# A gated delta-rule mixer: norm weight moved from the weights to the tokens, decay mask made additive, Silu in pairs, weight subtraction on GpSimd

## The chip, the cores and the metric

The kernel runs on one core of one Trainium2 chip. Its time is device microseconds of one execution of the whole program; the figure compared is the median over the timed executions. The core has TensorE (PE, matrix multiply, with a separate row for its weight loads, PEld), VectorE (DVE), ScalarE (ACT), GpSimd (POOL) and SyncE (SP, which here issues DMAs).

## What is computed

One inference step of a two-layer decoder for 1040 prompt tokens (16 of them learned meta tokens) and 8 single-token samples. Layer A is a gated delta-rule mixer and a convolutional feed-forward, layer B a latent attention and another feed-forward. The change is in the mixer of layer A:

```python
h = rmsnorm(x, a_norm_pre)                      # y * w, w one weight per channel
proj = h @ w_in                                 # q, k, v (each through conv4 and silu), z, a, b
gc = cumsum(g)                                  # per chunk
decay = exp(where(causal, gc[:, None] - gc[None, :], -inf))
strict = where(i > j, (beta k) @ k.T * decay, 0)
u, w = triangular_solve(1 + strict, [beta v, beta k exp(gc)])
attn = (q @ k.T) * decay
# recurrence over chunks: v_new = u - w S;  o = q exp(gc) S + attn v_new;  S = S exp(g_last) + k_tail.T v_new
o = rmsnorm(o, a_out_norm) * silu(z);  out = o @ w_out
```

## The kernel before

All matrix products of activations and weights are done in three passes on split numbers: a high half rounded for TensorE and a low half, the rest. `wprep` (L155) loads a 1024x128 weight tile by DMA into one staging buffer, and `wsplit` (L141) multiplies it by the norm weight on GpSimd where a fold is asked for (L144), rounds it on ScalarE (L151) and subtracts on VectorE (L152) to get the low half. The tokens are normalised by their root mean square without the weight at the start (L215), turned channel-major and split in the same way (L219 to L224); they stay on the chip as xh and xl.

The mixer has 8 heads. For each head there are four weight tiles, k, v, q and z (numbers 1, 2, 0, 3 in the list `tiles`, L161), each projected for three pieces of the tokens of 280, 384 and 384 columns. The order in the list is k, v, q of a head and then z of the head before. `inproj` (L493) projects a tile into one of two PSUM buffers (L93), ScalarE copies it out, and for k, v, q VectorE adds the four taps of the convolution (L546). When the third piece is there, `silu` (L133) is called for that one tile: the scalar engine loads the Silu table (L135), runs it, and loads the table of logarithm and exponential again (L131).

The z tiles of the heads but the last lie in a pool with a single buffer (L383, L507):

```python
zp = es.enter_context(tc.tile_pool(name="gz", bufs=1, reuse_waits="tile"))
...
y = zp.tile([P, T], F32, tag="z", name="z")
```

`chunks` (L560) does what a head needs before the recurrence, in nine chunks of 116 tokens in groups of three. It loads the cumulated decay of all tokens of a chunk on every partition (GC), and makes E, the decay matrix: subtract the own column and take the minimum with zero on VectorE (L581, once per chunk), exponential on ScalarE (L582, once per group), and multiply by the upper triangular mask of ones on GpSimd (L583). Then come the products of keys (L601) and U (L604), whose diagonal blocks go to DRAM and back. The blocks of 32 are inverted by substitution in 31 steps of two small VectorE instructions, a product and a difference (L658, L660), each waiting for the one before; the result goes over DRAM into X, is turned (L668 to L670), and the rest of the head's products follow from L680 on.

`recur` (L734) walks the nine chunks of a head in order. Per group of three it normalises the output and turns it (L770 to L778), multiplies by z (L782), and after the last group it does the 8 samples, which read the first columns of z at L825 ("og8"). That is the last reader of the z buffer. The outputs go to DRAM and are multiplied by the output weights at the end (`tail_a`, `outp`).

The streams are merged by a position number (`merge`, L834): head h's projections stand at h to h+1, its chunks at h+0.65 to h+1.9, its recurrence at h+1.9 to h+2.55, and the instructions are traced in that order. The framework then fixes the order of each engine's instructions when it compiles: earlier traced work first, among what it takes to be ready by its own estimate of times and of free buffers. A buffer is given to a new tile only when the last reader of the old one has been placed, wherever that reader was traced. In the run each engine takes its instructions strictly in that fixed order. `keep_in_program_order` pins an instruction behind the one traced before it on its engine.

Of the kernel before, what the change touches and what calls it, by code (L numbers as in the profile page):

```python
# [20 lines left out]
P = 128  # L21
# [40 lines left out]
def tile_step(ctx: ExitStack, tc: tile.TileContext, I, O, stop=None):  # L62
# [41 lines left out]
    def rsqrt(dst, src, scale, n=P):  # L104
        """dst = (src * scale + EPS)^-0.5"""
        A.activation(dst, src, AF.Ln, bias=epst[:n], scale=scale)
        A.activation(dst, dst, AF.Exp, scale=-0.5)
# [9 lines left out]
    # per-channel vectors as columns  # L117
# [15 lines left out]
    def silu(*ts):  # L133
        for t in ts:
            A.activation(t, t, AF.Silu)  # L135
        act_set()
# [4 lines left out]
    def wsplit(pool, st, kt, m, fold, tag, out=None):  # L141
# [10 lines left out]
        V.tensor_tensor(lo, st, hi, op=ALU.subtract)  # L152
        return hi, lo

    def wprep(pool, src, kt, m, fold=None, tag="w", out=None):  # L155
        st = pool.tile([P, KT * P], F32, tag=tag + "s", name="ws", bufs=1)[:, :kt * m].rearrange("p (k m) -> p k m", k=kt)
        SP.dma_start(st, src)
        return wsplit(pool, st, kt, m, fold, tag, out)
# [3 lines left out]
    for h in range(H):  # L162
        tiles += [(h, 1), (h, 2), (h, 0)] + ([(h - 1, 3)] if h else [])
# [3 lines left out]
    def prep(n):  # L167
        if n < len(tiles) and n not in prepped:
            h, ti = tiles[n]
            col = 1024 * ti + P * h  # L170
            prepped[n] = wprep(wg, I["a_w_in"][0, :, col:col + P].rearrange("(k p) m -> p k m", p=P), KT, P, fold="a_pre")

    A.preload_act_table_set("natural_log_exp_and_others")
    with tc.tile_pool(name="init", bufs=2, reuse_waits="tile") as ip, \
# [4 lines left out]
        def params(spec, conv):  # L179
            r0 = r = 8 if len(vcol) else 0  # L180
# [4 lines left out]
            if conv:  # L185
                A.dma_start(arow, I["a_conv_w"][0].rearrange("j (t p) -> (j t) p", p=P))
            pt = ipp.tile([P, 2, P], F32, name="pt", bufs=1)
            PE.transpose(pt[:, 0, :r], rows[:r, :], ident[:r, :r])
            V.tensor_copy(vec[:, r0:r], pt[:, 0, r0:r])
            if conv:  # L190
                PE.transpose(pt[:, 1, :96], arow, ident[:96, :96])
                V.tensor_copy(acv, pt[:, 1, :96])

        # tokens to channel-major, normalised
        for bi, (t0, n) in enumerate(BLK):
            xt = ip.tile([P, D], F32, name="xt", bufs=4)
            load_tokens(xt, bi)
            if bi == 1:
                params([("a_pre", I["a_norm_pre"][0], 8)], False)
# [3 lines left out]
            elif bi == 8:  # L203
# [6 lines left out]
                ], True)  # L210
# [4 lines left out]
            V.tensor_scalar(xt[:n], xt[:n], ss[:n], None, op0=ALU.mult)  # L215
# [19 lines left out]
    def stat(pp, aps, n, dst, dim):  # L235
        """dst[p, t] = (sum over channels / dim + eps)^-0.5 on every partition."""
# [10 lines left out]
    def boundary(pp, wide, c, wname, split=True, halves=False, store=False):  # L247
        """x <- x + acc * rstd * w for one chunk, kept in acc and, as halves, in xh and xl; the old x is in them or in x_d."""
# [51 lines left out]
    def outp(w, src_d, groups, pool, p0, p1, first=False, skip=0, ob=4):  # L300
        """Shares of an output projection, summed in acc, without the first skip tokens; a group is its heads and where
        their weights go."""
# [45 lines left out]
    # ------------------------------------------------------------------ layer A mixer  # L348
# [1340 lines left out]
```

## Time and profile before

| | us |
|---|---|
| median of 3 runs | 3347.21 |
| lowest and highest | 3346.63, 3354.2 |
| span of the profiled execution, first to last instruction | 3338.6 |
| median less that span | 8.6 |

The runs give no separate time for the profiled execution, so its span stands for it; the 8.6 us are what lies around the instructions. Times in the rows below are microseconds from the start of the span. The mixer runs from 0 to about 850 us, and the feed-forward of layer A follows. TensorE's own busy time is counted from modelled ends of pipelined matmuls. The chain that ended last is given by the page as TensorE 77%, VectorE 14%, DMA 3%, issue 3%, ScalarE 2%, GpSimd 1%.

### The profile page before, as it was taken

How to read it: one execution, taken by the hardware profiler on the slowest of the kernel's cores; microseconds unless marked ns; L12 is line 12 of the kernel's file. 1: busy time of each engine (PE TensorE's matmuls, PEld its weight loads, DVE VectorE, ACT ScalarE, POOL GpSimd, SP SyncE). 2: the span in 40 equal slices, each digit the busy share in tenths (PEclk: the TensorE clock that was granted, in tenths of full speed). 3: DMA queues.
4: the chain of work that ended last, by engine and by line, in shares of the span. 5: the costliest groups of instructions: out<-in, count | busy, mean ns of one | idle time of the engine just before them, and what ended most of it. 6: DMA issues, size and time to landing. Idle time of an engine off the chain costs nothing.

```text
span 3338.6 us, 52527 instructions
## 1 busy us (share of the span) xinstructions
PE 3151.7 (94%) x20846; PEld 2874.7 (86%) x20846; DVE 2031.4 (61%) x4139; ACT 1255.9 (38%) x2541; POOL 860.2 (26%) x1013
## 2 busy tenths in 40 slices
PE   7999999999899999999888999999998999999997
PEld 6888888888699999999877888856677999999996
DVE  4877777766854555555666666544457455655556
ACT  4656555663432222222334444433224322222223
POOL 1432222210442223222431001112104323322322
PEclk9999999999899999999999999999999999999999
DMA  3222222236311111111121000255432111111111
GB/s 109 59 72 71 59 64 69 69 105 184 93 52 39 52 51 45 46 39 55 48 79 39 25 19 27 65 214 195 155 107 77 52 45 45 45 41 56 45 39 65
DMA packets 267649, 235.08 MB, mean 70 GB/s; under 512 B 57918, under 2 KB 246596, under 8 KB 263284
## 3 DMA queue, kind: packets, MB, share of 16 engines
q1 hardware_dynamic: 260224, 189.69, 19.7%
q0 software_dynamic: 6912, 41.95, 3.4%
q8 instruction: 164, 2.69, 0.3%
q14 instruction: 81, 0.66, 0.1%
q10 hardware_dynamic: 268, 0.09, 0.0%
HBM read 198.84 MB, written 33.40 MB: 70 GB/s over the span
## 4 chain that ended last, share of the span: by engine, by line
PE 77%; DVE 14%; DMA 3%; issue 3%; ACT 2%; POOL 1%; SPq 0%; ACTq 0%; DVEq 0%; POOLq 0%
PE fps L228 9%; PE fps L229 9%; PE fps L227 9%; PE fdn L228 5%; PE fdn L227 5%; PE fdn L229 5%; PE psu L227 2%; PE psu L229 2%; PE po L1409 2%; PE psu L228 2%; PE dscr L1494 2%; DVE acc L287 2%; DVE xs L660 1%; DVE tm L658 1%; PE psop L227 1%
## 5 line engine op out<-in xcount | busy, mean ns | idle before, releaser
L144 POOL TENSOR_TENSOR ws<-ws,vec 128x1024 f32<-128x1024 f32 (+1 forms) x127 | 247.6, 1950 | 433.4 <-DMA ws<-in_f_w_up_dram 173.2
L228 PE MATMUL fps<-xfl,wh 128*128 128x384 f32 (+1 forms) x1056 | 343.7, 326 | 8.3 <-POOL xfl L295 8.3
L227 PE MATMUL fps<-xfh,wh 128*128 128x384 f32 (+1 forms) x1056 | 341.7, 324 | 8.0 <-ACT xfh L293 7.0
L228 PE MATMUL fps<-xbl,wh 128*128 128x384 f32 (+1 forms) x1056 | 342.5, 324 | 6.1 <-POOL xbl L295 6.1
L229 PE MATMUL fps<-xfh,wl 128*128 128x384 f32 (+1 forms) x1056 | 342.4, 324 | 0.0
L227 PE MATMUL fps<-xbh,wh 128*128 128x384 f32 (+1 forms) x1056 | 340.6, 323 | 1.1 <-ACT xbh L293 0.5
L229 PE MATMUL fps<-xbh,wl 128*128 128x384 f32 (+1 forms) x1056 | 340.2, 322 | 0.0
L966 DVE TENSOR_TENSOR fu<-fps,RS 128x384 f32<-128x384 f32 x176 | 98.1, 557 | 386.7 <-PE fps L229 386.2
L151 ACT CAST wh<-ws 128x1024 fp32r<-128x1024 f32 (+1 forms) x144 | 148.0, 1028 | 488.1 <-PE fps L228 374.0
L227 PE MATMUL fdn<-gh,dh 128*128 128x384 f32 (+1 forms) x960 | 315.8, 329 | 0.0
L228 PE MATMUL fdn<-gl,dh 128*128 128x384 f32 (+1 forms) x960 | 311.9, 325 | 0.0
L229 PE MATMUL fdn<-gh,dl 128*128 128x384 f32 (+1 forms) x960 | 309.0, 322 | 0.0
L1044 DVE TENSOR_TENSOR acc<-acc,fdn 128x384 f32<-128x384 f32 (+1 forms) x432 | 216.9, 515 | 108.5 <-PE fdn L229 107.7
L227 PE MATMUL psu<-xah,wh 128*128 128x384 f32 (+1 forms) x768 | 261.2, 340 | 11.3 <-ACT u L533 7.0
L228 PE MATMUL psu<-xal,wh 128*128 128x384 f32 (+1 forms) x768 | 259.1, 337 | 0.4 <-DVE xal L223 0.4
L229 PE MATMUL psu<-xah,wl 128*128 128x384 f32 (+1 forms) x768 | 258.7, 337 | 0.7 <-DVE wl L152 0.7
L975 DVE SCALAR_TENSOR_TENSOR fy<-fu,fcv,fy 128x1064 f32<-128x1064 f32 x176 | 238.6, 1358 | 7.5 <-ACT fy L973 7.3
L152 DVE TENSOR_TENSOR wl<-ws,wh 128x1024 fp32r<-128x1024 f32 (+1 forms) x144 | 173.7, 1206 | 70.3 <-ACT wh L151 70.1
L228 PEld LDWEIGHTS fps<-xfl,wh 128*128 128x128 f32 x1056 | 200.8, 190 | 10.7 <-POOL xfl L295 10.5
L227 PEld LDWEIGHTS fps<-xfh,wh 128*128 128x128 f32 x1056 | 200.4, 190 | 9.4 <-ACT xfh L293 7.9
L228 PEld LDWEIGHTS fps<-xbl,wh 128*128 128x128 f32 x1056 | 199.6, 189 | 8.0 <-POOL xbl L295 7.7
L229 PEld LDWEIGHTS fps<-xfh,wl 128*128 128x128 f32 x1056 | 200.8, 190 | 0.4
(963 smaller groups left out, 7857.1 us busy)
## 6 DMA issues: line engine op xcount, KB each, us to landing
ws<-in_f_w_up_dram SPq DMA_DIRECT2D x88, 512.0 KB
ds<-in_f_w_down_dram SPq DMA_DIRECT2D x44, 512.0 KB
ws<-in_a_w_in_dram SPq DMA_DIRECT2D x32, 512.0 KB
xt<-in_x_prompt_dram SPq DMA_DIRECT2D x16, 512.0 KB
of<-og_d SPq DMA_DIRECT2D x32, 192.0 KB
xr<-x_d SPq DMA_DIRECT2D x16, 384.0 KB
GC<-gcd SPq DMA_DIRECT2D x24, 174.0 KB
Ss<-in_state_delta_S_dram SPq DMA_DIRECT2D x8, 512.0 KB
```

What stands on the lines that cost most here:

```text
L144: G.tensor_tensor(st, st, bc(fo, [P, kt, m]), op=ALU.mult)
L151: A.copy(hi, st)
L152: V.tensor_tensor(lo, st, hi, op=ALU.subtract)
L227: PE.matmul(ps, wh, ah, start=start, stop=False)
L228: PE.matmul(ps, wh, al, start=False, stop=False)
L229: PE.matmul(ps, wl, ah, start=False, stop=stop)
L287: V.scalar_tensor_tensor(a_[:, k + j, :], a_[:, k + j, :], vc(wname, k + j), res[j], op0=ALU.mult, op1=ALU.add)
L966: V.tensor_tensor(u[:, 18 + t0:18 + t0 + n], ps[:, :n], RS[:, t0:t0 + n], op=ALU.mult)
L975: V.scalar_tensor_tensor(y, u[:, j:j + LW], fcv[:, l, j, tl:tl + 1], y, op0=ALU.mult, op1=ALU.add)
L1044: V.tensor_tensor(acc[c][:, m, :], acc[c][:, m, :], ps[:, :n], op=ALU.add)
L1409: PE.matmul(po[:, :nq], vt[:kk, kb, P * (h % 2):P * (h % 2) + P], pT[:kk, j, :nq], start=(kb == 0), stop=(kb == i))
L1494: PE.matmul(sc[32 * j:32 * j + 32, :], ql[:, k, b, :], cT[:, j, :], start=(k == 0), stop=False, tile_position=(0, 32 * j))
```

## The change

The norm weight is loaded once on every partition (512 KB) and multiplied into the tokens together with the root mean square. The weight tiles are no longer multiplied, and for the mixer's projections the low half is subtracted on GpSimd. The two calls for parameters become one. The decay mask is added (0 or -1e30) on GpSimd before the exponential, and the own column is subtracted as the bias of the exponential, which is therefore run once per chunk; VectorE has no part in it. The tiles are ordered k, z of the head before, v, q. Silu is called for two tiles at a time, the later tile first, and the second pinned behind the first. The first head's q and the last z are alone. A negated copy of gc is kept in place of gc. Comments were removed as well.

```diff
     def silu(*ts):
-        for t in ts:
-            A.activation(t, t, AF.Silu)
+        for i, t in enumerate(ts):
+            ins = A.activation(t, t, AF.Silu)
+            if i:
+                tc.keep_in_program_order(ins)
         act_set()
...
         A.copy(hi, st)
-        V.tensor_tensor(lo, st, hi, op=ALU.subtract)
+        (sub or V).tensor_tensor(lo, st, hi, op=ALU.subtract)
...
-        tiles += [(h, 1), (h, 2), (h, 0)] + ([(h - 1, 3)] if h else [])
+        tiles += [(h, 1)] + ([(h - 1, 3)] if h else []) + [(h, 2), (h, 0)]
...
-            prepped[n] = wprep(wg, I["a_w_in"][0, :, col:col + P]..., KT, P, fold="a_pre")
+            prepped[n] = wprep(wg, I["a_w_in"][0, :, col:col + P]..., KT, P, sub=G)
...
+        pre = ip.tile([P, D], F32, name="pre", bufs=1)
+        A.dma_start(pre, I["a_norm_pre"][0].partition_broadcast(P))
...
-                params([("a_pre", I["a_norm_pre"][0], 8)], False)
                 prep(0)
...
-            V.tensor_scalar(xt[:n], xt[:n], ss[:n], None, op0=ALU.mult)
+            V.scalar_tensor_tensor(xt[:n], xt[:n], ss[:n], pre[:n], op0=ALU.mult, op1=ALU.mult)
...
-    triu = gp.tile([C, C], F32, name="triu")
-    SP.dma_start(triu, I["c_triu"])
+    umask = gp.tile([C, C], F32, name="umask")
+    SP.dma_start(umask, I["c_umask"])
...
-    gc = gp.tile([C, NCK, H], F32, name="gc")
+    ngc = gp.tile([C, NCK, H], F32, name="ngc")
...
-        wh, wl = wprep(wg, I["a_w_in"][0, :, 4096:4112]..., KT, 16, fold="a_pre",
+        wh, wl = wprep(wg, I["a_w_in"][0, :, 4096:4112]..., KT, 16,
...
+        triu = rp.tile([C, C], F32, tag="tm", name="triu")
+        SP.dma_start(triu, I["c_triu"])
...
+        gc = part(440, C, 72).rearrange("p (a b) -> p a b", b=H)
         V.tensor_copy(gc, ps1[:C])
+        V.tensor_scalar(ngc, ps1[:C], -1.0, None, op0=ALU.mult)
...
+    waiting = []
+
+    def finished(t, alone=False):
+        waiting.insert(0, t)
+        if len(waiting) == 2 or alone:
+            silu(*waiting)
+            waiting.clear()
...
                 if c == 2:
-                    silu(y)
+                    finished(y, h == H - 1)
...
             if c == 2:
-                silu(y[:, :LC])
+                finished(y[:, :LC], h == 0 and ti == 0)
...
+            G.tensor_tensor(E[:, gs, :], GC[:C], umask.unsqueeze(1).to_broadcast([C, 3, C]), op=ALU.add)
             for i in range(3):
                 k = 3 * g + i
-                V.tensor_scalar(E[:, k, :], GC[:C, i, :], gc[:, k, h:h + 1], 0.0, op0=ALU.subtract, op1=ALU.min)
-            A.activation(E[:, gs, :], E[:, gs, :], AF.Exp)
-            G.tensor_tensor(E[:, gs, :], E[:, gs, :], triu.unsqueeze(1).to_broadcast([C, 3, C]), op=ALU.mult)
+                A.activation(E[:, k, :], E[:, k, :], AF.Exp, bias=ngc[:, k, h:h + 1])
             A.activation(GC, GC, AF.Exp)
...
+    c["c_umask"] = np.where(np.triu(np.ones((C, C))) > 0, 0.0, -1e30).astype(f)
```

## Rows read from the trace of the kernel before

**Rows 1.** The page, part 1: busy microseconds of each engine, share of the span, instructions

```profile
PE 3151.7 (94%) x20846; PEld 2874.7 (86%) x20846; DVE 2031.4 (61%) x4139; ACT 1255.9 (38%) x2541; POOL 860.2 (26%) x1013
```

**Rows 2.** Busy time by stretch: one head of the first mixer, after the column line

```profile
core 0: us, PE busy (x) PEld busy (x) DVE busy (x) ACT busy (x) POOL busy (x), PEclk, DMA share, GB/s
439.00:527.00 88.00, 80.11 (x625) 74.03 (x626) 65.57 (x196) 51.19 (x145) 24.62 (x40) 0.96 0.25 67
```

**Rows 3.** Waits of TensorE, 90 to 700 us: total, times, longest

```profile
PE psot L778 <- DVE tm L658: 19.6, 4, 4.9
...
PE psr L680 <- DVE Tt L668: 5.3, 2, 3.0
PE pskt L596 <- DVE Kh L592: 5.0, 5, 2.0
PE pso L823 <- DVE o L820: 3.6, 5, 0.8
PE psot L778 <- DVE on L775: 3.4, 2, 2.3
```

**Rows 4.** Groups by line, 0 to 870 us: xcount, busy us, mean ns, idle before

```profile
L144 POOL TENSOR_TENSOR ws<-ws,vec 128x1024 f32<-128x1024 f32 (+1 forms) x36 | 68.9, 1914 | 185.3 <-DMA ws<-in_a_w_in_dram 87.3 <-DMA og_d<-og 37.1 <-DVE acc L336 36.8
L660 DVE TENSOR_TENSOR xs<-xs,tm 108x84 f32<-108x84 f32 (+23 forms) x248 | 66.8, 269 | 2.8
...
L152 DVE TENSOR_TENSOR wl<-ws,wh 128x1024 fp32r<-128x1024 f32 x38 | 46.3, 1220 | 16.8 <-ACT wh L151 16.7
...
L135 ACT ACT_TABLE_LOAD x32 | 41.1, 1283 | 0.6
...
L581 DVE TENSOR_SCALAR E<-GC,gc 116x116 f32<-116x116 f32 x72 | 32.9, 464 | 0.2 <-DMA GC<-gcd 0.2
...
L583 POOL TENSOR_TENSOR E<-E,triu 116x348 f32<-116x348 f32 x24 | 27.3, 1136 | 12.0 <-ACT E L582 12.0
...
L770 ACT ACTIVATE sqo<-pso 116x128 f32<-116x128 f32 x72 | 19.9, 276 | 31.8 <-PE pso L760 31.2
...
L582 ACT ACTIVATE E<-E 116x348 f32<-116x348 f32 x24 | 11.7, 487 | 18.6 <-DVE E L581 18.6
...
L215 DVE TENSOR_SCALAR xt<-xt,ss 128x1024 f32<-128x1024 f32 (+1 forms) x9 | 6.6, 745 | 5.5 <-ACT ss L107 5.5
```

**Rows 5.** Groups by line, 900 to 1300 us, in the feed-forward

```profile
L975 DVE SCALAR_TENSOR_TENSOR fy<-fu,fcv,fy 128x1064 f32<-128x1064 f32 x48 | 65.3, 1366 | 3.2 <-ACT fy L973 3.1
...
L1007 POOL TENSOR_TENSOR gl<-fy,gh 128x1040 fp32r<-128x1040 f32 x12 | 29.2, 2435 | 3.8 <-ACT gh L1004 3.8
```

**Rows 6.** Timeline of VectorE in that head: start, us, instruction

```profile
453.09 0.19 DVE L658 TENSOR_TENSOR tm<-ins,xs 108x31 f32<-108x31 f32 x1
...
458.18 1.98 DVE L581 TENSOR_SCALAR E<-GC,gc 116x116 f32<-116x116 f32 x1
...
484.73 0.21 DVE L825 SCALAR_TENSOR_TENSOR og<-pso,vec,z 128x8 f32<-128x8 f32 x1
...
490.82 0.16 DVE L660 TENSOR_TENSOR xs<-xs,tm 108x11 f32<-108x11 f32 x1
...
500.54 0.46 DVE L668 STREAM_TRANSPOSE Tt<-X 32x288 f32<-32x288 f32 x1
```

**Rows 7.** Timeline of GpSimd at the same place

```profile
458.14 1.94 POOL L144 TENSOR_TENSOR ws<-ws,vec 128x1024 f32<-128x1024 f32 x1
```

**Rows 8.** Timeline of TensorE there, idle time before in brackets

```profile
467.74 0.81 PE L778 MATMUL psot<-ident,on 116*128 116x116 f32 x3 [4.82 <-DVE tm L658]
...
468.60 0.43 PE L228 MATMUL psu<-xal,wh 128*128 128x280 f32 x1
...
473.52 0.29 PE L229 MATMUL psu<-xah,wl 128*128 128x280 f32 x1
```

**Rows 9.** Timeline of ScalarE there

```profile
455.67 0.37 ACT L533 COPY u<-psu 128x272 f32<-128x272 f32 x1
...
490.31 0.39 ACT L522 COPY z<-psu 128x280 f32<-128x280 f32 x1 [1.13 <-PE psu L229]
```

More of the change, by code (lines that the diff above doesn't have):

```diff
@@ L139, in vc, with wsplit @@
         return vec[:, vcol[nm] + k:vcol[nm] + k + 1]
-    def wsplit(pool, st, kt, m, fold, tag, out=None):
+    def wsplit(pool, st, kt, m, fold, tag, out=None, sub=None):
         if fold is not None:
@@ L151, in wsplit, with wprep @@
         A.copy(hi, st)
-        V.tensor_tensor(lo, st, hi, op=ALU.subtract)
+        (sub or V).tensor_tensor(lo, st, hi, op=ALU.subtract)
         return hi, lo
-    def wprep(pool, src, kt, m, fold=None, tag="w", out=None):
+    def wprep(pool, src, kt, m, fold=None, tag="w", out=None, sub=None):
         st = pool.tile([P, KT * P], F32, tag=tag + "s", name="ws", bufs=1)[:, :kt * m].rearrange("p (k m) -> p k m", k=kt)
         SP.dma_start(st, src)
-        return wsplit(pool, st, kt, m, fold, tag, out)
+        return wsplit(pool, st, kt, m, fold, tag, out, sub)
     heads = [{} for _ in range(H)]
@@ L170, in prep @@
             col = 1024 * ti + P * h
-            prepped[n] = wprep(wg, I["a_w_in"][0, :, col:col + P].rearrange("(k p) m -> p k m", p=P), KT, P, fold="a_pre")
+            prepped[n] = wprep(wg, I["a_w_in"][0, :, col:col + P].rearrange("(k p) m -> p k m", p=P), KT, P, sub=G)
     A.preload_act_table_set("natural_log_exp_and_others")
@@ L177, in tile_step, with params @@
         arow = ip.tile([96, P], F32, name="arow", bufs=1)
-        def params(spec, conv):
-            r0 = r = 8 if len(vcol) else 0
+        def params(spec):
+            r = 0
             for nm, ap, k in spec:
@@ L184, in params @@
                 r += k
-            if conv:
-                A.dma_start(arow, I["a_conv_w"][0].rearrange("j (t p) -> (j t) p", p=P))
+            A.dma_start(arow, I["a_conv_w"][0].rearrange("j (t p) -> (j t) p", p=P))
             pt = ipp.tile([P, 2, P], F32, name="pt", bufs=1)
             PE.transpose(pt[:, 0, :r], rows[:r, :], ident[:r, :r])
[L189 to L192, printed above, removed]
+            V.tensor_copy(vec[:, 0:r], pt[:, 0, 0:r])
+            PE.transpose(pt[:, 1, :96], arow, ident[:96, :96])
+            V.tensor_copy(acv, pt[:, 1, :96])
+        pre = ip.tile([P, D], F32, name="pre", bufs=1)
+        A.dma_start(pre, I["a_norm_pre"][0].partition_broadcast(P))
         for bi, (t0, n) in enumerate(BLK):
@@ L209, in tile_step @@
                     ("a_out", I["a_out_norm"][0], 1), ("b_qa", I["b_q_a_norm"][0], 3), ("kv_a", I["kv_a_norm"], 2),
-                ], True)
+                ])
             sqt = ip.tile([P, D], F32, name="sqt", bufs=1)
@@ L420, in gates @@
         G.memset(abT[:, T:], 0.0)
-        wh, wl = wprep(wg, I["a_w_in"][0, :, 4096:4112].rearrange("(k p) m -> p k m", p=P), KT, 16, fold="a_pre",
+        wh, wl = wprep(wg, I["a_w_in"][0, :, 4096:4112].rearrange("(k p) m -> p k m", p=P), KT, 16,
                        out=lambda: hp.tile([P, KT * 16], F32R, tag="E", name="wab", bufs=2))
```

## Prediction

> **What bounds the kernel now.** I read the page's busy line first: TensorE is busy for 94% of the span and VectorE for 61% [rows 1]. Taken alone, that says that only work of TensorE counts. But the change touches no matmul, so its room is TensorE's idle time in the mixer. The second view, busy time by stretch, shows it for one head: 80.11 of 88 us busy, VectorE 65.57, ScalarE 51.19, GpSimd 24.62, at a mean granted clock of 0.96 [rows 2]. Between 90 and 700 us there are seven such periods of 85 to 88 us with about 7 us idle in each; the row shown is typical. The third view, the waits of TensorE there, names what ends this idle time: VectorE, nearly always. Its five rows sum to 19.6 + 5.3 + 5.0 + 3.6 + 3.4 = 36.9 us [rows 3].
>
> The largest, 4 waits of 4.9 us, is the same event in four heads, and the timelines show its cause. VectorE works through the substitution from 453.09 to 490.82, 38 us [rows 6]. Its 62 instructions of 0.27 us are 16.6 us of that [rows 4]; the rest is other work that sits between them. Some of it is not even work: a 0.27 us subtraction of the decay takes 1.98 us from 458.18, while GpSimd multiplies a weight tile for 1.94 us from 458.14 [rows 6, 7]. The two engines hold each other up. TensorE has by then projected ahead as far as its buffers go, stops, and resumes at 467.74 after 4.82 us with the turned output of the recurrence [rows 8]. It then runs at 1.2 GHz: a matmul of 280 columns lasts 0.43 us at 468.60 and 0.29 us at 473.52 [rows 8]. These 4.9 us at half speed lose some 2.4 us more.
>
> After the substitution come the way over DRAM and the turn at 500.54 [rows 6], then the products of that head, and the next head's keys, which feed the next substitution. This loop from head to head takes about as long as a period. So the mixer is held by TensorE's work and by this loop at once, and the loop's long part is VectorE's.
>
> **The change part by part.**
>
> *VectorE, decay.* Nine instructions per head go, 72 x 0.464 = 32.9 us in all, 4.1 us per head [rows 4]. GpSimd's multiplication by the mask (1.14 us per group) becomes an addition of the same shape at the same price, earlier in the chain. ScalarE runs 72 exponentials of 116 columns in place of 24 of 348. No row shows one with a bias column; the nearest, a square of 116x128, is 0.276 us [rows 4], and the bounds are half of that and the 0.487 us of the long one. I take 0.28: 20.2 against 11.7 us, +1.1 us per head, on an engine with 37 idle us per head.
>
> *VectorE, weights.* Four subtractions per head go: 4 x 1.22 = 4.9 us [rows 4]. Together VectorE loses 9.0 of 65.6 us per head, and about two thirds of that lies in the 38 us stretch.
>
> *GpSimd, weights.* The multiplication of 1.91 us goes [rows 4], a subtraction of two full tiles comes. The same operation with the same types takes 2.44 us for 1040 columns [rows 5], so 2.40 for 1024: +0.5 us a tile, +2 us per head, on an engine with 63 idle. The bounds: it could hold VectorE for all of 4 x 2.40 = 9.6 us per head where the multiplication could for 4 x 1.91 = 7.6, so at most 2 us of the 9 go back. The low half is needed a whole tile after its load, so the longer step is hidden; if a GpSimd queue filled up before it, the third pass of each product would wait, at up to 2.4 us a tile.
>
> A rule of the skill speaks against this part. The Trainium skill, GPSIMD Engine Reference, Engine selection, puts elementwise work on VectorE because GpSimd is about 2x slower with two inputs, and its Key points say that the two share their SBUF interfaces. By that rule the subtraction at 2 x 1.22 = 2.44 us would take VectorE out for twice as long as VectorE needs itself, and the gain of 4.9 us per head would become a loss of 4.9. What it leaves out is the multiplication that goes at the same time.
>
> *ScalarE, table loads.* 32 calls of Silu load two tables each; the row shows one of the two groups, the other (L131) is its twin [rows 4]. With pairs there are 17 calls: one pair and one single in the first head, two pairs in each of seven, one at the end. 30 loads of 1.283 us go, 38.5 us or 4.8 per head. None is on TensorE's path directly; I count nothing, and what it gives is a shorter way for the chain of the recurrence.
>
> *Order k, z, v, q.* Queries are needed at position h + 1.06 and now finish at h + 1.0 instead of h + 0.75; the keys wait for z's Silu, at h + 0.5 instead of h + 0.25, needed at h + 0.68. Both fit. The z buffer does not. z of head h - 1 is now written from h + 0.25, and head h - 2 reads the only buffer until h + 0.45. In the trace the projection after k is copied out from 455.67 [rows 9]; in the new order that is z. Its buffer is free only behind the L825 at 484.73 [rows 6]; today's z follows 5.6 us later at 490.31 [rows 9]. Two projected pieces fit into PSUM, then TensorE has no projection to do, and behind z stand v, q, the next k and, through the pair, this head's keys. With today's times TensorE would stop at 462.9, where it stops now, and wait until 484.7: 21.8 us, less some 3 us of the recurrence's own matmuls.
>
> How early L825 comes decides. Between 462.9 and 484.7 VectorE does about 12 convolution steps of v and q at 0.53 to 0.61 us and a weight subtraction of 1.22, none of which stand there any more, since v and q come later: 8 us. The decay's instructions and what GpSimd holds up before 462.9 give 3.5, the slow clock 2.4, stuck single instructions 2. That brings L825 to about 469. Less the 3 us of own matmuls, the stop is some 3 us. Since the loop over the heads is shortened by 12 to 15 us, recurrences also start earlier relative to the projections. I take 2 us for each of the six heads with this conflict (z of heads 1 to 6): +12 us. The bounds are 0 and 6 x 18.8 = 113.
>
> *Start.* Tokens are scaled by a two-operand instruction: by its nearest row 1.37 us for 1064 columns [rows 5] against 0.745 [rows 4], 9 x 0.6 = 5.4 us of VectorE, and 512 KB more are loaded. In exchange the first weights wait for no parameters and no multiplication of 1.9 us. Bounds +5.4 and -4; I take -1. *End* (700 to 870 us): the relief of VectorE for the last head's chain, between 0 and 9 us; I take -2.
>
> **The sum**, against the profiled span of 3338.6 us: the four long waits with their slow clock, 4 x (4.9 + 2.4) = -29; of the other VectorE waits, 17.3 us, half: -9; the z buffer +12; start -1; end -2. That is -29 us, a span of 3310. The median of the runs is 8.6 us above the profiled span, so 3318.
>
> **The rivals.** (1) *The z buffer decides, slower.* Then the long waits do not go, they change their name: L825 comes at about 476, the stop is 10 us instead of 4.8 and is followed by the slow clock as today. That is six heads x (10 + 2.4) = 74 in place of 29, and the rest of the sum (-12) stays: +33, 3380. For it: one buffer, two readers two heads apart, six times over. Against it: most of what delays L825 now leaves that stretch. The point from which it decides: the gains are 41 us, 6.8 per head, so a stop of more than about 4.5 us with its slow clock turns the sign.
>
> (2) *Nothing comes of it.* TensorE's order stays what holds it, the subtraction on GpSimd holds VectorE up by what was saved, and the idle time of 7 us per head only moves: 3347, within 10. For it: 91% busy in the stretch. Against: VectorE ends nearly every wait. (By the Trainium skill's page on GpSimd named above it would even be a loss.) If the pairs were split by other functions, and the loads stayed 64, that too would change nothing, as ScalarE is idle for 37 us per head.
>
> (3) *All of the idle time goes.* TensorE is left with its own work at full clock: seven periods x (7 idle + 2) = -63, 3284.
>
> By the Trainium skill, Trainium Kernel Development and Optimization, Performance Expectations, a trace's matmul time is a poor measure and weight-load time a better one. The rows have 74.03 us of loads in 88 us [rows 2], 14 us idle instead of 8; by it the third rival's limit would lie at 7 x 14 = 98 us.
>
> **Chances and range.** The forecast 0.52, rival 1 0.22, rival 2 0.16, rival 3 0.10. A measurement of this kernel tells about 0.3% (10 us) from no change. The forecast itself spans 3300 to 3335, from a z wait of 0 to one of 5 us per head. Of 0.52 I give 0.02 to a gain under 10 us, and rival 1 puts 0.02 near 3350: faster 0.60, same 0.18, slower 0.22. The range reaches to half of rival 3 and to nearly half of rival 1: 3290 to 3373.
>
> **What would show it.** Right: the row of TensorE's waits for the turned output behind L658 gone or under 5 us; substitution within 30 us; VectorE near 57 us per head; 34 table loads of Silu and back; GpSimd's subtraction near 2.4 us; the last read of z within 22 us of the first copy of k's successor. Wrong: a TensorE idle stretch of over 8 us in each head ended by the copy of z (L522 or its new line), a granted clock under 0.95 there, periods of 88 us or more. Then rival 1 holds, and the step that fails is the z wait of 2 us.

## The result and the profile after

The changed kernel takes 3401.62 us (median of 4 runs, 3398.88 to 3408.62) against 3346.92 for the kernel before (3341.02 to 3354.2): 1.0165 times as long, 95% interval 1.0146 to 1.0185. The forecast was 3318, the upper end of its range 3373. The profiled execution has a span of 3406.9 us, 68.3 more than before. That is more than the 55 us between the medians: the execution profiled after is the slowest of its four, and the one profiled before is by its span quicker than any of its four. (In the changed kernel a run of 3408.62 us has a span of 3406.9, so of the 8.6 us that the time before lists around the instructions only some 2 lie there.)

The busy line of the page, the counterpart of [rows 1], shows a little less work of VectorE and no more of GpSimd:

```profile
PE 3182.6 (93%) x20845; PEld 2899.8 (85%) x20845; DVE 2028.0 (60%) x4035; ACT 1227.5 (36%) x2560; POOL 860.5 (25%) x1012
```

The first products behind a head's substitution (psr, L680 before, L694 now) divide the span; a period below is the time from one head's psr to the next. By the trace they start at 157, 245, 327, 414, 502, 589, 675 and 747 us before, and at 167, 247, 338, 433, 528, 624, 719 and 810 now. So the start lost 10 us, the six periods between head 0 and head 6 lost 34 (553 against 519), the last period 19 (91 against 71). The first of the six is 8 us shorter than before (80 against 88), so the other five lost 42. From the last psr to the first matmul of the feed-forward it is 92 us instead of 93, and behind it the changed kernel is 6 us longer. 10 + 34 + 19 - 1 + 6 = 68. The ends of this row by source line:

```profile
L680 PE MATMUL psr<-Tt,U x144: 191/191/212, 157.0 to 749.3; 32*32 32x32 f32 x144
```

```profile
L694 PE MATMUL psr<-Tt,U x144: 191/191/212, 166.8 to 812.5; 32*32 32x32 f32 x144
```

One head of the changed kernel by stretch, with the columns of [rows 2]. TensorE has hardly more busy time than there, but in 95 us instead of 88, and at a granted clock of 0.93 instead of 0.96. VectorE, which was forecast near 57 us in a head, has 65.14, as much as before (65.57):

```profile
455.00:550.00 95.00, 82.56 (x625) 75.91 (x624) 65.14 (x184) 47.04 (x145) 24.81 (x41) 0.93 0.24 62
```

Over the six periods VectorE fell from 388.89 to 378.73 us, 1.7 us per head where 9 had been counted (before, then after):

```profile
157.00:675.50 518.50, 476.89 (x3743) 439.62 (x3744) 388.89 (x1184) 305.37 (x855) 148.34 (x234) 0.97 0.26 69
```

```profile
166.80:719.50 552.70, 480.05 (x3633) 438.78 (x3634) 378.73 (x1090) 276.10 (x859) 142.15 (x228) 0.93 0.24 62
```

The waits of TensorE from 90 to 700 us, which answer to [rows 3]. The wait behind the substitution (psot <- tm) is gone, as forecast. Others of the same size stand in its place:

```profile
PE psot L792 <- DVE on L789: 20.3, 5, 4.1
PE pso L837 <- DVE o L834: 15.1, 5, 3.1
PE psot L792 <- DVE frq L649: 8.5, 5, 1.7
PE pskt L610 <- DVE Kh L606: 8.3, 12, 1.9
PE psu L230 <- ACT u L548: 6.3, 3, 3.2
```

What these waits mean is seen in three timelines of one head. First TensorE (start, length, idle time before in brackets). It projects until 498.75 and takes the next projection up at 512.81. In these 14 us it has only the recurrence's own small products, most of them late by VectorE (the stop in [rows 8] was 4.82 us). The matmul behind it lasts 0.69 us where one of the same form took 0.34 before the stop: the granted clock is 1.00 from 490 to 498 us and 0.50 from 512.8 to 518, so behind the stop TensorE runs at 1.2 GHz instead of 2.4.

```profile
498.75 0.34 PE L232 MATMUL psu<-xah,wl 128*128 128x384 f32 x1
503.15 0.81 PE L792 MATMUL psot<-ident,on 116*128 116x116 f32 x3 [4.07 <-DVE on L789]
...
511.79 0.27 PE L837 MATMUL pso<-ident,o 8*128 8x8 f32 x1 [3.02 <-DVE o L834]
512.81 0.69 PE L230 MATMUL psu<-xah,wh 128*128 128x384 f32 x1 [0.74 <-ACT z L537]
```

VectorE reads the old z for the last time at 512.10 (L839, the L825 of [rows 6]):

```profile
512.10 0.23 DVE L839 SCALAR_TENSOR_TENSOR og<-pso,vec,z 128x8 f32<-128x8 f32 x1 [0.22 <-PE pso L837]
```

And ScalarE copies the new z out directly behind it, two pieces at once (in [rows 9] this copy came 5.6 us after the last reader):

```profile
512.36 0.78 ACT L537 COPY z<-psu 128x280 f32<-128x280 f32 x2
```

The same pair stands in six heads: last readers at 225, 323, 417, 512, 607 and 703, first copies at 226, 323, 418, 512, 608 and 703. The waits' table charges this stop to the small products, because they end its pieces. The line that names z has 3.7 us. A stop of 14 us has to be read from where the projection itself ends and begins.

The groups by line up to 870 us answer to [rows 4]. Most prices came near the forecast: 2.42 us for the subtraction (2.40), 34 table loads of Silu and back (34), 1.54 for the scaling (1.37); the exponential with bias took 0.38 where 0.28 was taken. The substitution's instructions keep their mean:

```profile
L155 POOL TENSOR_TENSOR wl<-ws,wh 128x1024 fp32r<-128x1024 f32 x32 | 77.4, 2419 | 206.8 <-ACT wh L154 206.8
L674 DVE TENSOR_TENSOR xs<-xs,tm 108x84 f32<-108x84 f32 (+23 forms) x248 | 65.5, 264 | 5.5
...
L597 ACT ACTIVATE E<-E,ngc 116x116 f32<-116x116 f32 x72 | 24.1, 379 | 9.6 <-POOL E L594 9.6
L594 POOL TENSOR_TENSOR E<-GC,umask 116x348 f32<-116x348 f32 x24 | 22.1, 930 | 6.1 <-DMA GC<-gcd 6.1
L136 ACT ACT_TABLE_LOAD x17 | 21.8, 1283 | 0.3
...
L218 DVE SCALAR_TENSOR_TENSOR xt<-xt,ss,pre 128x1024 f32<-128x1024 f32 (+1 forms) x9 | 13.7, 1539 | 13.6 <-ACT ss L107 13.6
```

One subtraction of GpSimd in the changed kernel, 487.11 to 489.49:

```profile
487.11 2.38 POOL L155 TENSOR_TENSOR wl<-ws,wh 128x1024 fp32r<-128x1024 f32 x1 [6.02 <-ACT wh L154]
```

And VectorE beside it. This product of 116x3 elements takes 0.16 us in the median of its 24 executions; here it takes 1.96 and ends at 489.51, with the subtraction:

```profile
487.55 1.96 DVE L787 TENSOR_TENSOR f<-f,frq 116x3 f32<-116x3 f32 x1
```

The Trainium skill, SBUF — State Buffer, section SBUF: two separate sides, has a rule for this: GpSimd and a VectorE instruction with two SBUF inputs use one port pair under an exclusive lock, held for the whole instruction. The trace agrees: VectorE's instruction started second, and the two end 0.02 us apart.

### The profile page after: what moved, and what is told of

It is laid out like the page before. It is cut to its first block, busy times and chain, and to the rows that moved or that the text cites. A ratio compares the mean times of both kernels' runs of the same rounds, so it can differ in the third digit from the quotient of the medians.

```text
span 3406.9 us, 52407 instructions
## 1 busy us (share of the span) xinstructions
PE 3182.6 (93%) x20845; PEld 2899.8 (85%) x20845; DVE 2028.0 (60%) x4035; ACT 1227.5 (36%) x2560; POOL 860.5 (25%) x1012
## 4 chain that ended last, share of the span: by engine, by line
PE 74%; DVE 15%; ACT 4%; issue 3%; DMA 3%; POOL 1%; SPq 0%; DVEq 0%; ACTq 0%; POOLq 0%
PE fps L231 9%; PE fps L232 9%; PE fps L230 9%; PE fdn L231 5%; PE fdn L230 4%; PE fdn L232 4%; PE po L1423 2%; PE psu L231 2%; PE dscr L1508 2%; PE psu L230 2%; PE psu L232 2%; DVE acc L290 2%; PE psop L230 1%; PE psop L232 1%; PE psop L231 1%
## 5 line engine op out<-in xcount | busy, mean ns | idle before, releaser
L147 POOL TENSOR_TENSOR ws<-ws,vec 128x1024 f32<-128x1024 f32 x94 | 189.7, 2018 | 322.2 <-DMA ws<-in_f_w_up_dram 205.3
L231 PEld LDWEIGHTS fps<-xfl,wh 128*128 128x128 f32 x1056 | 200.7, 190 | 10.7 <-POOL xfl L298 10.4
L230 PEld LDWEIGHTS fps<-xbh,wh 128*128 128x128 f32 x1056 | 200.7, 190 | 1.7 <-ACT xbh L296 0.9
L232 PEld LDWEIGHTS fps<-xbh,wl 128*128 128x128 f32 x1056 | 201.1, 190 | 0.3
```

The costliest lines, as they stand in the source:

```text
L147: G.tensor_tensor(st, st, bc(fo, [P, kt, m]), op=ALU.mult)
L230: PE.matmul(ps, wh, ah, start=start, stop=False)
L231: PE.matmul(ps, wh, al, start=False, stop=False)
L232: PE.matmul(ps, wl, ah, start=False, stop=stop)
```

## The experiments

The kernel before ran beside each group of experiments: 3345.28, 3346.41, 3348.28, 3347.32 and 3350.31 us. All ratios are to it. Differences between runs of different groups carry a few us, as this kernel's own medians do.

**The order alone.**

```diff
-        tiles += [(h, 1), (h, 2), (h, 0)] + ([(h - 1, 3)] if h else [])
+        tiles += [(h, 1)] + ([(h - 1, 3)] if h else []) + [(h, 2), (h, 0)]
```

> The kernel before, with the order k, z, v, q alone; Silu one tile at a time, decay, weights and norm weight as before. Theory Z (the single z buffer makes the difference): the first copy of z waits for the last read of the z two heads back, and since VectorE still has all of its old work, that read comes no earlier than in the changed kernel. TensorE idles about 10 us in each of six heads ahead of L825, a head's period grows from 87 to about 97 us: 3400 to 3430 us. Rival G (the subtraction on GpSimd holds VectorE up): the order alone costs nothing, 3337 to 3357 us. Rival P (the pairs delay keys behind z's Silu): no pairs here, 3337 to 3357 us.

3388.31 us, 1.0135 (1.011 to 1.0161). The order alone costs 43 us, the periods go from 87 to 93 or 94 us from head 2 on, and z is copied behind its last reader as in the changed kernel. The wait behind the substitution is gone here too, and the substitution of the head in [rows 6] takes 27 us in place of 38, though VectorE still has all of its old work. So the order alone brings about two of the forecast's signs, without the cause that it gave for them. The waits between 90 and 700 us bear nearly the changed kernel's names:

```profile
PE psot L778 <- DVE on L775: 20.4, 10, 4.4
PE pso L823 <- DVE o L820: 18.1, 6, 3.1
```

**All but the order.** The changed kernel with the old order; pairs are then keys with values, queries with z.

> The changed kernel with the old order k, v, q, z and the pairs that follow from it (k with v, q with z); all else as changed. Theory Z: no z waits for its buffer, as in the kernel before; VectorE's 9 us per head show, periods of 80 to 83 us instead of 95, the start still some 5 to 10 us late: 3300 to 3325 us. Rival G: the subtraction on GpSimd is still there, so it stays near 3400 us. Rival P: keys still wait for another tile's Silu, so it stays above 3370 us.

3369.7 us, 1.0083 (1.0057 to 1.0109), so the other parts together are a loss too. The substitution took 29 us instead of 38 (473.0 to 501.6), yet the period is 89. That is 45 us above theory Z's range and at the edge of theory P's. VectorE's waits only changed their names again:

```profile
PE psot L792 <- DVE on L789: 17.8, 5, 3.6
PE psu L230 <- ACT u L548: 14.5, 7, 5.9
PE psr L694 <- DVE Tt L682: 13.1, 6, 2.6
```

**z in parts, three runs on the changed kernel.** z of a head in four tiles, so that a copy waits for the reader of its own columns only:

```diff
-                        y = zp.tile([P, T], F32, tag="z", name="z")
+                        y = [(0, NS, zp.tile([P, NS], F32, tag="z8", name="z8", bufs=2))]
+                        for g in range(3):
+                            a0, a1 = NS + 3 * C * g, min(NS + 3 * C * (g + 1), T)
+                            y.append((a0, a1, zp.tile([P, a1 - a0], F32, tag=f"z{g}", name=f"z{g}")))
```

> The changed kernel, order and pairs included, with z kept in three tiles by the groups of the recurrence that read them, and its 8 sample columns in a small tile with two buffers; each is free as soon as its own reader is done, some 10 to 30 us before the last read. It costs three more copies and some more Silu instructions per head on ScalarE. Theory Z: the idle time ahead of L825 goes or falls under 3 us, periods of 80 to 85 us: 3300 to 3330 us. Rivals G and P, and a rival O (the order itself, q late, not the buffer): near 3400 us.

3403.27 us, 1.0184 (1.0156 to 1.0211), but it tells nothing of the buffer: the parts' Silus stood apart, and one head (431 to 526 us) has 13 table loads where the changed kernel has four. With the first two weight tiles subtracted on VectorE besides (`sub=G if n > 1 else V`):

> As the kernel with z in three tiles, and the first two weight tiles subtract on VectorE again, so that GpSimd holds nothing while the tokens are scaled at the start. If GpSimd's hold on VectorE is what makes the start late (a scaling of 1.27 us took 3.04 beside a subtraction on GpSimd), the first substitution starts some 5 us earlier and the time is 4 to 6 us under the kernel with z in three tiles; if the longer scaling and the added load are it, no difference.

3400.87 us, 1.0171 (1.0145 to 1.0196), psr of head 0 at 165. With all subtractions on GpSimd again and the parts' Silus held together (`tc.keep_in_program_order` on the first too):

> The changed kernel with z of a head in four tiles (one for the 8 decode columns with two buffers, one for each group of three chunks), so that a copy of the new z waits only for the reader of its own columns, and with all Silus of a call kept together behind its last input. In the run before with z in parts the Silus had been placed apart, with about 9 table loads per head where 2 to 4 are needed, so it told nothing of the z buffer. Theory Z (the one z buffer sets the 95 us period): the first copies of z come some 10 us ahead of the last reader, periods fall to 88 to 90 us, 3360 to 3370 us in all. Theory O (the order itself, by what stands later in TensorE's stream, and not the buffer): copies come earlier, but periods stay at 93 to 96 us and the time within 10 us of 3401. Between them (3375 to 3390) both take part.

3385.78 us, 1.0113 (1.0092 to 1.0133): 16 us below the changed kernel, with copies some 20 us ahead of the last reader and periods still 90 to 94. The buffer has a part in it: 16 of the 32 us that the old order gives back (3402 to 3370, with other pairs).

**The other parts alone.** Norm weight in the tokens, low halves on VectorE:

> The kernel before with the norm weight multiplied into the tokens alone: GpSimd's multiplication of each weight tile goes, the subtraction for the low halves stays on VectorE; decay, Silus and order as before. Theory S (the start is late because of the scaling by the weight row, not because of the subtraction on GpSimd): the first matmul of the recurrence (head 0) comes at 165 to 168 us as in the changed kernel, 10 us later than before, and the periods of 87.5 us stay: 3350 to 3358 us. Theory G (the subtraction on GpSimd makes the start late): the first at 155 to 158 us, time 3335 to 3348. My prediction had priced the start at -1 us, and the missing multiplications on GpSimd at a relief of VectorE of up to 2 us per head, which by it would give 3330 to 3340.

3312.25 us, 0.9896 (0.988 to 0.9913): 34 us faster, more than any theory had it, with periods of 83 us and psr of head 0 at 151. The decay:

> The kernel before with the decay by an additive mask on GpSimd and exponentials with bias alone. VectorE loses 9 instructions of 0.464 us per head, all ahead of the substitution. My prediction's step (VectorE's relief shortens the four long waits): with 4.1 of its 9 us per head, about half of the -38 us, so 3320 to 3335 us. Rival V (VectorE's relief buys nothing, since TensorE takes the same idle time at another place): 3338 to 3352 us, substitution shorter by 4 us or more, TensorE idle per head within 1 us of 7 us.

3346.27 us, 0.9993 (0.9978 to 1.0008): nothing. Rival V holds: TensorE's wait behind L658's counterpart fell from 19.6 to 8.4 us, and that for the normed output rose from 3.4 to 16.0. The pairs of Silus in the old order:

> The kernel before with Silu in pairs alone, in the old order: keys with values, queries with z. 30 table loads of 1.28 us go from ScalarE. Theory P (the pair holds the keys back until the values are there, and with them the substitution): from the first turn of the keys to the first substitution step 36 to 40 us instead of 28, periods of 89 us, 3352 to 3362 us. Prediction's step (a table load is never on TensorE's path, the pair costs nothing): 3335 to 3350 us.

3361.85 us, 1.0047 (1.0031 to 1.0064): 15 us lost, the time that theory P has. From a head's first product of the keys (pskk) to its substitution it is 36 us from head 4 on (432 to 468 there), and 28 before. But the trace does not show its reason, keys held back by their partner: head 4's keys pass their Silu at 401 us, 29 before their first turn. What stands in the way is the pair of z and q with its two table loads. ScalarE takes 4.7 us for it in the middle of the squares (sq) for the norm of the same keys:

```profile
442.42 0.28 ACT L567 ACTIVATE sq<-pstr 116x128 f32<-116x128 f32 x1
...
444.11 1.08 ACT L135 ACTIVATE z<-z 128x1048 f32<-128x1048 f32 x1
445.09 1.08 ACT L135 ACTIVATE q<-q 128x1072 f32<-128x1072 f32 x1
...
447.49 0.28 ACT L567 ACTIVATE sq<-pstr 116x128 f32<-116x128 f32 x1
```

From head 4 on this pair comes behind the first product of the keys, in the heads ahead of it before. No run moved it.

**The subtraction.** The kernel with the norm weight in the tokens, with one word more:

```diff
-            prepped[n] = wprep(wg, I["a_w_in"][0, :, col:col + P]..., KT, P)
+            prepped[n] = wprep(wg, I["a_w_in"][0, :, col:col + P]..., KT, P, sub=G)
```

> The norm weight in the tokens as in the run before (3312 us) plus the subtraction of the low halves on GpSimd; decay, Silus and order as in the kernel before. Theory H (what GpSimd does with two inputs holds VectorE, so the 34 us came from the missing multiplications of 1.9 us and go back with the subtractions of 2.4 us): 3335 to 3355 us, the start as in the run before, periods of 86 to 88 us instead of 83, single substitution steps of 0.5 to 2 us beside a subtraction. Rival R (VectorE rid of 36 instructions of 1.22 us gains, GpSimd has room): 3295 to 3312 us, periods of 83 us or less.

3372.35 us, 1.0074 (1.0051 to 1.0097): not the 34 us go back but 60. The low halves are not simply late: between 90 and 700 us no wait of TensorE names the subtraction. Where the time goes is seen in VectorE's groups by form from 90 to 700 us. First the kernel without `sub=G`:

```profile
L546 DVE SCALAR_TENSOR_TENSOR k<-u,acv,k 128x384 f32<-128x384 f32 x42 | 27.4, 653 | 4.8 <-ACT k L544 4.6
L546 DVE SCALAR_TENSOR_TENSOR v<-u,acv,v 128x384 f32<-128x384 f32 x42 | 25.6, 610 | 0.0
...
L830 DVE TENSOR_SCALAR vr<-vr,kqz 128x128 f32<-128x128 f32 x48 | 11.5, 282 | 25.0 <-DMA vr<-vd 25.0
```

Then with it. The same instructions are up to half as long again:

```profile
L546 DVE SCALAR_TENSOR_TENSOR k<-u,acv,k 128x384 f32<-128x384 f32 x42 | 38.3, 912 | 5.0 <-ACT k L544 4.8
...
L546 DVE SCALAR_TENSOR_TENSOR v<-u,acv,v 128x384 f32<-128x384 f32 x42 | 31.8, 758 | 0.4 <-ACT v L544 0.4
...
L830 DVE TENSOR_SCALAR vr<-vr,kqz 128x128 f32<-128x128 f32 x48 | 18.1, 420 | 5.5 <-DMA vr<-vd 5.3
```

Over the six periods VectorE was rid of 23 subtractions, 28.0 us, and is 15 us busier than without that word (first without, then with it):

```profile
151.30:650.70 499.40, 476.60 (x3745) 441.37 (x3744) 364.90 (x1184) 306.31 (x858) 105.67 (x212) 0.97 0.28 71
```

```profile
163.70:693.50 529.80, 481.23 (x3704) 438.24 (x3704) 379.49 (x1161) 311.37 (x859) 159.18 (x237) 0.96 0.26 67
```

So its other instructions are 43 us longer, beside 59 us of subtractions on GpSimd. Many of them stand in chains for which TensorE waits. The changed kernel with the word taken out:

> The changed kernel with the subtraction of the low halves back on VectorE, all else as changed. Theory H (GpSimd's subtraction holds VectorE up): 3365 to 3385 us, the periods 91 to 93 us instead of 95. Rival R (the subtraction on GpSimd is a relief): 3405 to 3430 us, VectorE 5 us busier per head. If the z buffer alone sets the period, neither shows: 3395 to 3407 us.

3371.61 us, 1.0082 (1.0047 to 1.0116): 30 us back, and psr of head 0 at 153 instead of 167. VectorE, which now does the subtractions itself, is less busy over the six periods than without them (370 us against 379):

```profile
152.80:688.60 535.80, 476.38 (x3642) 440.60 (x3643) 369.61 (x1115) 277.71 (x859) 95.50 (x208) 0.92 0.25 65
```

The norm weight with the decay:

> Norm weight in the tokens and the decay by mask and bias, subtraction on VectorE, old order, single Silus. The decay alone was worth 0 within 0.15%. Theory V (TensorE takes the same idle time elsewhere whatever VectorE is spared): 3306 to 3318 us, periods of 83 us. Rival: with the loop over the heads shorter than before, VectorE's 4.1 us per head now count: 3280 to 3300 us.

3331.04 us, 0.9948 (0.9929 to 0.9967): here the decay costs 19 us. TensorE now waits 9.1 us for copies u of ScalarE and 11.3 us behind exponentials E, where it waited 2.1 for the copies and under 1.2 for exponentials. But these waits replace others: the six periods together take 501 us where they took 499. The loss stands at the start (psr of head 0 at 157 instead of 151) and in the last period (81 instead of 71 us). Why it does was not tested.

**The order on the faster kernel.** Norm weight in the tokens and the new order, with one z buffer and with z in parts:

> Norm weight in the tokens and the order k, z, v, q, single Silus, one whole z buffer: the partner of the run with z in parts (3350 us, periods of 86 us). Theory Z (the buffer is a good part of the order's cost): 3365 to 3385 us, periods of 89 to 92 us, first copies of z right behind the last reader. If the buffer costs nothing once VectorE is relieved: 3345 to 3355 us, periods of 86 us.

> Norm weight in the tokens (3312 us alone) plus the order k, z, v, q, with single Silus, and with z of a head in four tiles so that a copy of the new z waits only for the reader of its own columns; the z parts' Silus stand together. The order alone had cost 42 us on the kernel before. Theory Z (the z buffer is the whole of that): 3310 to 3325 us, periods of 83 to 85 us, first copies of z at least 8 us ahead of the last reader. Theory O (it is the order itself: what is projected beside the substitution, values and queries coming later): 3340 to 3360 us, periods of 87 us and more, though the copies come ahead of the last reader. Between (3326 to 3339) both.

3375.17 us, 1.0082 (1.0057 to 1.0107), and 3350.37 us, 1.0005 (0.9988 to 1.0023). In the second the copies do run ahead; here the first of head 5's at 545.50 (ScalarE), the last reader at 568.03 (VectorE):

```profile
545.50 0.43 ACT L534 COPY z<-psu 128x8 f32<-128x8 f32 x2
```

```profile
568.03 0.23 DVE L837 SCALAR_TENSOR_TENSOR og<-pso,vec,z 128x8 f32<-128x8 f32 x1
```

So the buffer is 25 of the 63 us that the order costs here; 38 are the order's own. The last head in the old order, and the control of z in parts in the old order throughout:

> The run with norm weight, new order and z in parts (3350 us), but the last head's tiles in the old order (keys, values, queries, then z of head 6). Theory L (in the new order the last head's recurrence starts later, as values and queries stand behind z of head 6): from the first matmul of head 6's recurrence to that of head 7's 70 to 75 us instead of 86, and 3333 to 3340 us. Rival: the last period is as long as before, 3345 to 3355 us, and the loss sits elsewhere.

> Norm weight in the tokens (3312 us), z of a head in four tiles, old order k, v, q, z: a control for what the parts cost by themselves. If they cost nothing: 3308 to 3317 us, and the 32 to 38 us that the order costs with z in parts are the order's own. If they are the cost: 3330 to 3345 us. Against that: ScalarE has 3 more copies and 3 more Silus in a head, some 3 us, with 30 us idle.

3344.18 us, 0.9981 (0.9962 to 0.9999): the last period went from 86 to 82 us only, the one ahead of it from 86 to 90, and the feed-forward's first projection begins no earlier (870 us in both), so theory L falls. And 3313.4 us, 0.9885 (0.9844 to 0.9925): the parts cost nothing.

**The rest of GpSimd's two-input work.** On the kernel with the norm weight in the tokens, `G.tensor_tensor` to `V.tensor_tensor` in L583 and L724, or in L583, L631, L723 and L724:

> As the run with four operations on VectorE, but only the two that fall into the substitution: the mask's product and the product of the keys with the decay to the end, 6 instructions per head. Strong form of theory H: 3298 to 3310 us, substitution steps of 0.7 to 0.9 us beside GpSimd gone. Rival: 3312 to 3330 us.

> Norm weight in the tokens (3312 us), and all four two-input operations of the mixer's heads that GpSimd still has (mask, queries by decay, two products of the keys; 12 instructions of 0.83 to 1.2 us per head) on VectorE. Theory H in its strong form (each such operation on GpSimd takes VectorE out for its whole time, so VectorE, which needs 0.4 to 0.55 us for each, is better off): 3295 to 3310 us. Rival (only those that meet VectorE's burst matter, and 12 more instructions in VectorE's queue wait there for TensorE): 3315 to 3345 us.

Two: 3310.98 us, 0.9868 (0.9825 to 0.991), not to be told from 3312. Four: 3295.97 us, 0.9828 (0.9788 to 0.9867), the fastest kernel of this study, 106 us below the changed one. On GpSimd the four took, 90 to 700 us:

```profile
L583 POOL TENSOR_TENSOR E<-E,triu 116x348 f32<-116x348 f32 x24 | 28.7, 1195 | 14.7 <-ACT E L582 14.7
L631 POOL TENSOR_TENSOR q<-q,GC 128x348 f32<-128x348 f32 x24 | 22.2, 926 | 54.8 <-PE psqk L628 54.8
L724 POOL TENSOR_TENSOR KL<-Kh,etl 116x384 f32<-116x384 f32 x24 | 21.2, 908 | 26.1 <-PE p L759 26.1
L723 POOL TENSOR_TENSOR KG<-Kh,egc 116x384 f32<-116x384 f32 x23 | 19.1, 832 | 67.1 <-PE psw L731 63.2 <-POOL KG L723 3.9
```

On VectorE:

```profile
L724 DVE TENSOR_TENSOR KL<-Kh,etl 116x384 f32<-116x384 f32 x24 | 13.2, 549 | 0.0
L723 DVE TENSOR_TENSOR KG<-Kh,egc 116x384 f32<-116x384 f32 x23 | 12.6, 554 | 1.3 <-PE psw L731 0.2
L583 DVE TENSOR_TENSOR E<-E,triu 116x348 f32<-116x348 f32 x24 | 12.4, 515 | 0.0
L631 DVE TENSOR_TENSOR q<-q,GC 128x348 f32<-128x348 f32 x24 | 12.3, 512 | 0.0
```

VectorE is busier by 14 us over the six periods (379 against 365), though the four cost it 38 us of its own there, and TensorE waits for it less: its largest wait between 90 and 700 us is

```profile
PE psu L227 <- ACT u L533: 2.9, 3, 2.1
```

and the periods are 78 us. The changed kernel with these four and the subtraction on VectorE:

> The changed kernel with the subtraction and the four other two-input operations of the mixer's heads on VectorE. By theory H: 3372 us (with the subtraction on VectorE) less the 16 us that the four were worth on the norm weight alone, 3345 to 3362 us; the z buffer still sets the period, 89 us or more, first copies of z right behind the last reader. Rival: with nothing held up, the last reader of z comes early enough and the order costs nothing: 3290 to 3310 us, periods of 80 us.

3338.76 us, 0.9962 (0.9943 to 0.9981): 63 us below the changed kernel, and 6 below the range of theory H. The copies of z still stand behind the last reader, in periods of about 87 us, and 43 us remain to the same kernel with single Silus, the old decay and the old order.

## Why the prediction was wrong

By runs that add one step to the next: 3347, norm weight alone 3312 (-34), with the decay 3331 (+19), with pairs and order, two parts at once, 3372 (+41), with the subtraction on GpSimd 3402 (+30). The sizes hold for this sequence only: the decay alone is worth nothing on the kernel before, and the subtraction costs 60 us straight behind the norm weight.

*The step that failed* is the relief of VectorE, 9.0 us per head of which "at most 2 us go back". Over the six periods 1.7 us per head are left of it. Three things made that up. The multiplications on GpSimd had held VectorE for 24 us in these periods (389 to 365 us by the norm weight alone), 4 us per head. The subtractions on GpSimd hold it for 36 us (changed kernel) to 43 (norm weight), 6 to 7 us per head: more than VectorE had needed to do them itself (4.7). And the decay's nine instructions, priced at 4.1 us, took 2.1 us off VectorE alone and nothing on the faster kernel (365 us with and without it). Part of their price was GpSimd's hold, and that fell on their neighbours: with the decay alone the substitution's product went from 266 to 317 ns. Rows 6 and 7 had shown it, 1.98 us on an instruction of 0.27. In time, taking the subtraction off GpSimd gives 30 us of the changed kernel's 55 back. The rule of the Trainium skill that I set aside (GPSIMD Engine Reference, Engine selection) had the sign right; by my working of it the loss was 4.9 us per head, some 39 us.

That the norm weight alone gains 34 us, near the -38 of the four long and the other waits, is luck. The sum had those 38 us from instructions taken off VectorE, and the kernel that gains 34 has them all. Its long waits fell from 19.6 to 12.9 us only. That less of GpSimd's hold is the whole of the gain was not shown, since the weights also come earlier without the multiplication (psr of head 0 at 151 us instead of 157).

*The order.* This is the second step that failed. The z wait of 2 us per head was named as the step on which all hangs, and it went as rival 1 has it: stops of 14 us ahead of a slow clock, periods of 95 us. Undone alone it gives 32 us of the 55 back. In time the buffer is 16 us (in the changed kernel) to 25 (on the norm weight), against the +12 of the sum. As large or larger is what the sum did not have at all: with the buffer out of the way the order still costs 37 us on the norm weight (3350 against 3313, both with z in parts) and 16 in the changed kernel (3386 against 3370, with other pairs). "Both fit" was read from positions, and nothing here bears it out.

*Pairs.* Counted as nothing; alone they lose 15 us, by the trace through the pair of z and q in the middle of the keys' norm. With the order the partner of the keys is z itself, so keys also wait for the buffer: in the changed kernel the last head's keys pass their Silu at 714 us, 5 before psr of the head ahead; in the kernel before at 627, 48 before. That is not what makes the last period 19 us longer, though, which the sum had at -2 with the end: with the order alone, single Silus and keys at 666 us, it is 91 us as well.

*Decay.* Nothing alone, +19 on the faster kernel. The 38 us stretch of the substitution did shrink to 24, but not for the forecast's reason: the decay alone takes it to 34 or 35 us, the order alone to 27. Rival 2's reading was right here: the idle time moved.

*Start.* -1 was forecast, +10 came. It is the subtraction: psr of head 0 goes from 151 to 164 us when it is added to the norm weight, and from 167 to 153 when it is taken out of the changed kernel. The scaling by two operands, which TensorE waits for by up to 10.2 us at the start, is won back later, as the kernel with the norm weight alone has it too (10.7) and starts early. Two tiles on VectorE were too few to show this.

*Slips in the working.* None of them turns the forecast. "VectorE, nearly always" passed over the second line of the waits' table, which waits for ScalarE:

```profile
PE psu L227 <- ACT u L533: 6.0, 6, 1.6
```

The second of the periods is 82 us and not 85 to 88; 72 x 0.464 is 33.4; and by its own terms the chances are 0.20 for the same time and 0.20 for a slower one.

*What stays open*: why the order costs what it does beside the buffer. The two kernels with z in parts that differ in the order alone show where. The six periods take 514 us instead of 493, with waits of TensorE of 36.7 us instead of 20.5 and a granted clock of 0.95 instead of 0.98; its waits for the normed output are 13.6 us against 7.4. The last period is 12 us longer, and there TensorE has more of its own work (623 matmuls against 566). This fits values' and queries' projections and convolutions that now stand there, but no run moved them alone. Nor is it settled why two operations moved to VectorE gave nothing measurable and four gave 16 us: with two, the trace already has periods of 80 us instead of 83 and a mixer that ends 5 us earlier, and the 95% interval on its time is some 28 us wide.

## What to carry to other kernels

Charge a two-input elementwise operation on GpSimd to VectorE as well, wherever VectorE has work on a chain: idle time of GpSimd is not free room. In four pairs of runs here VectorE lost (or got back, where they went) between a third and three quarters of the length of such operations in the six periods: 24 of 68 us for the last four, 24 of 45 for the multiplications, 36 of 53 and 43 of 59 for the subtractions. Before an order of projections is changed, ask of each buffer that is written earlier when its last reader comes, and read a stop from where the stopped work ends and begins, since the waits' table puts it under other names. Try the parts of a bundled change alone: here one of them was worth 34 us, and the others hid it.

## What was not expected

A step of 0.61 us took 2.44 beside a subtraction on GpSimd that itself took 3.06 instead of 2.4 (norm weight with `sub=G`):

```profile
484.96 2.44 DVE L546 SCALAR_TENSOR_TENSOR v<-u,acv,v 128x384 f32<-128x384 f32 x1 [0.20 <-ACT v L544]
...
487.48 1.28 DVE L546 SCALAR_TENSOR_TENSOR v<-u,acv,v 128x384 f32<-128x384 f32 x1
```

```profile
483.92 3.06 POOL L152 TENSOR_TENSOR wl<-ws,wh 128x1024 fp32r<-128x1024 f32 x1 [4.48 <-ACT wh L151]
```

So GpSimd's instruction was longer too; of the 32 of this run 4 took over 2.6 us, where the median is 2.40. And the price of an operation is not its own: the means of L581 are 472 ns in the kernel before from 90 to 700 us, 330 without GpSimd's multiplications, 272 with the four others gone from GpSimd as well, for one and the same instruction. With the multiplications still there, the order alone brings it to 325: what counts is which instructions fall together.
